# Splitting the next stage's first weight whole before a joint, an output bias as a product, and a longer last run of the down products

## The chip, the cores and the metric

The kernel runs on one core of one Trainium2 chip. The metric is the device time of one execution in microseconds (us); lower is better. The core has a matrix engine (PE), a vector engine (DVE), a scalar engine (ACT), a general engine (POOL) and a queue that only issues transfers (SP). Each takes its own instructions strictly in order, and they wait for one another by semaphores.

## The reference, cut to what matters

One sequence of 256 tokens with 1024 channels passes through two blocks, each of depth two. What follows is cut to the residuals and the parts that the change touches.

```
def rglru_mixer(u, ...):
    ...
    out = (h * ybr) @ w_out + b_out
def conv_ffn(u, w_up, conv_w, conv_b, w_down):
    hcv = causal_dwconv(u @ w_up, conv_w, conv_b)          # 1024 -> 8192
    g, v = hcv[..., :D_FF], hcv[..., D_FF:]
    return (gelu(g) * v) @ w_down                          # 4096 -> 1024
def first_block(x, ...):
    for i in range(2):
        m = ssd_mixer(rmsnorm(x, norm_mix_pre[i]), ...) if i == 0 else rglru_mixer(...)
        x = x + rmsnorm(m, norm_mix_post[i])
        x = x + rmsnorm(conv_ffn(rmsnorm(x, norm_ffn_pre[i]), ...), norm_ffn_post[i])
def second_block(x, c, ...):
    for l in range(2):
        sh1, sc1, gt1, sh2, sc2, gt2 = split(silu(c) @ ada_w[l] + ada_b[l], 6)
        h = rms_norm(x, norm1_g[l]) * (1 + sc1) + sh1
        ...                                                # attention and delta net, merged by gates
        x = x + gt1 * (merged @ w_out[l])
        h = rms_norm(x, norm2_g[l]) * (1 + sc2) + sh2
        x = x + gt2 * (square(relu(h @ w_mlp1[l])) @ w_mlp2[l])
```

## The kernel before, in words

There are eight stages in a row: ssd, ffn0, lru, ffn1, mixer2_0, mlp2_0, mixer2_1, mlp2_1. Between two of them stands a joint, numbered here J1 (ssd to ffn0) to J7 (mixer2_1 to mlp2_1). The 256 tokens are two token tiles of 128, t0 and t1.

Every large product is made in float32 out of three products of split operands (`mm3`, L333 to L335): each factor is cut into a high part and a low part, and high by high, high by low and low by high are added up in PSUM. The weights stream from memory as blocks of 128 x 2048 (`raw`, loaded by SP). A half of a block is a granule: ACT makes its high part (`hi`, L432), DVE its low part (`lo`, L434), which needs the high one. Activations are split the same way (`yh` and `yl`, `xhh` and `xhl`, `hTh` and `hTl`).

A stage ends with its products into four accumulators, acc00 and acc01 for t0 (512 channels each) and acc10 and acc11 for t1. The joint then works on t0 first: residual (L543 to L551 for a normed one, L559 and L560 for a gated one), sum of squares on ACT (L497), inverse root on POOL (`n_ssv` L499, `n_ssr` L503), gain (L517), scale (L520 or L522), eight transposes on PE (`pT`, L531), split into `hTh` and `hTl`. Right behind, PE makes the first product of the next stage for t0 (`ph`, 24 matmuls, L333 to L335), while DVE, ACT and POOL do the same chain for t1. The weight of that first product has four granules, the list `self.ahead`, which `prefetch` splits.

In the two FFNs and the two MLPs `updown` runs over 32 channel tiles: an upward product (`pg` twice, or `pu` once), activation, and later the tile's down products into the accumulators; the products of the last `nl` tiles are made at the end, one accumulator after the other (`out_last`), so that t0's accumulators are done first.

The code is not executed as it stands. A list scheduler orders the instructions of each engine by their dependences and by the place in the code, and `self.after(late, early)` adds an order by hand. A code edit therefore moves instructions elsewhere on an engine's queue too.

Of the kernel before, what the change touches and what calls it, by code (L numbers as in the profile page):

```python
# [17 lines left out]
P = 128  # L18
# [8 lines left out]
# ---------------------------------------------------------------- host layout  # L27
def _chan(a):
    """[C] or [J, C] per-channel values -> [128, J * C / 128], channel = col * 128 + row."""
    a = np.asarray(a)  # L30
    a = a.reshape(-1, P)
    return a.T
# [18 lines left out]
def _kslab(w):  # L51
    """[1024, n] -> [128, 8 * n] with row k * 128 + p at [p, k, :]."""
    n = w.shape[1]
    return w.reshape(KD, P, n).transpose(1, 0, 2).reshape(P, KD * n)


def _ct(w):
    """[k * 128, c] -> [c / 128, 128, k * 128]: one block per 128 columns"""
    r, c = w.shape
    return w.reshape(r // P, P, c // P, P).transpose(2, 1, 0, 3).reshape(c // P, P, r)  # L60


def _pair(a, b=None):
    """blocks two by two: neighbours of a, or a's with b's"""
    if b is None:
        a, b = a[0::2], a[1::2]
    return np.ascontiguousarray(np.concatenate([a, b], 2))


def _nt(w, n):  # L70
    """[1024, c] -> [2 * c / n, 128, 4 * n]"""
    r, c = w.shape
    return np.ascontiguousarray(w.reshape(2, 4, P, c // n, n).transpose(3, 0, 2, 1, 4)).reshape(2 * c // n, P, 4 * n)


def _rt(w):
    """[r, 1024] -> [r / 256, 128, 2 * 1024]"""
# [108 lines left out]
# ---------------------------------------------------------------- kernel  # L186
class Kern:
    def __init__(self, tc, ctx, a, out, at):
# [20 lines left out]
        # the tables are there before the data  # L209
# [5 lines left out]
    def after(self, late, early):  # L215
        """late is issued after early"""
# [32 lines left out]
    def rowload(self, rp, name, eng=None):  # L249
        """one row of 1024 values on all partitions; name is a parameter row or (layer, row of its modulation)"""  # L250
# [5 lines left out]
    # ---- weights  # L256
    def load_par(self, name, eng=None):
        """the per-channel parameters of a stage"""
# [16 lines left out]
    def outpools(self, ctx, name, raw, hi=4):  # L275
        """a stage's own pools for the weights of its last product"""
        return self.pool(ctx, name + "r", raw), self.pool(ctx, name + "h", hi)

    def wload(self, name, i, pool=None, cuts=1):
        """block i of a weight"""  # L280
# [7 lines left out]
    def parts(self, name, i, shape=(8, P), pools=None):  # L288
        """the two halves of block i, each split: [128, *shape] high and low"""
# [9 lines left out]
    def gran(self, raw, shape, pool=None):  # L299
        """one split granule of a weight"""  # L300
# [5 lines left out]
    def ahead_of(self, gen, n):  # L306
        """the same items, each made n items earlier"""
# [22 lines left out]
    def mm3(self, ps, ah, al, bh, bl, first, last):  # L330
        """ps += (ah + al)^T (bh + bl)"""
# [5 lines left out]
    def proj_ch(self, ps, hl, hT):  # L337
        """channels on partitions: ps [128, 256] = w^T h"""
# [4 lines left out]
    def proj_tok(self, ps, hls, hT, t):  # L343
        """tokens on partitions: ps [128, n] = h[tile t] w"""
# [7 lines left out]
    def prefetch(self):  # L352
        """the weights of the next stage's first product"""
        if self.next_head:
# [3 lines left out]
            self.ahead, self.later = [next(self.ahead) for _ in range(2)], self.ahead  # L358

    def head(self, wk, hT, relu2=False, tag="up"):  # L360
        """the first 512 channels of a projection, made with tokens on partitions so that the first token tile
        goes ahead of the second, then transposed: four [128, 256] with channels on partitions"""
# [19 lines left out]
    # ---- small things  # L382
    def rsqrt(self, ss, n, scale, eps, c=""):
        """1 / sqrt(ss * scale + eps), [128, n]"""
# [19 lines left out]
    def softplus(self, x, n):  # L404
        """max(x, 0) + log1p(exp(-|x|)) in place, [128, n]"""
# [24 lines left out]
    def tosplit(self, src, h, l):  # L430
        """h, l = the two exact parts of src"""
# [4 lines left out]
    # ---- between two stages  # L436
    def joint(self, post, pre, first=None):
        """the residual after a stage and the normed, transposed and split input of the next one.
        post: (accumulators, gain row, bias row) for a normed residual, (accumulators, gate row) for a gated one.
        pre: gain row, shift row"""  # L440
        with ExitStack() as ctx:
            jp = self.pool(ctx, "jp", 1, "right")
            xs = []
            for t in range(2):
# [3 lines left out]
                if not post and not t:  # L448
                    # the gain's row goes to all partitions by a product
# [16 lines left out]
            for t in range(2):  # L466
# [8 lines left out]
                if pre:  # L475
                    xn = self.norm(jp, x, *pre_rows)
                    if not t and post:
                        for hl in self.later:
                            if len(post) == 2 or post[1] in ('mix_post1', 'ffn_post0'):
                                self.after(self.lo[-1], self.xg)  # L480
                            self.ahead.append(hl)
                    if t and post:
                        # the first token tile's products go ahead of the second's norm
# [7 lines left out]
    def rnorm(self, jp, halves, scale, eps, name):  # L491
        """1 / sqrt(sum of (scale * halves)^2 + eps)"""
# [13 lines left out]
    def norm(self, jp, x, grow, shrow=None):  # L506
        """rms norm of x times a gain row (plus a shift row)"""
# [17 lines left out]
    def to_chan(self, t, xn, hT):  # L525
        """transposed and split"""
# [8 lines left out]
    def add_normed(self, jp, x, acc, g, b):  # L535
        """x += rms norm of acc (+ bias row) times a gain row"""
# [16 lines left out]
    def add_gated(self, jp, x, acc, gt):  # L553
        """x += gate row * acc"""
# [7 lines left out]
    def out_tok(self, acc, yh, yl, hi, lo, first, last):  # L562
        """acc[t][n] += y[tile t]^T w[:, n half]"""
# [9 lines left out]
    def out_last(self, acc, todo):  # L573
        """the last products into acc, one accumulator after the other"""
# [5 lines left out]
    def conv(self, out, src, taps, shifts, bias=None):  # L580
        """out[:, i] = bias + sum_j taps[j] * src[:, i + shifts[j]], zeros outside; taps[-1] has shift 0"""
# [11 lines left out]
    # ---- first block: SSD  # L593
    def ssd(self, prev):
        nc, tc = self.nc, self.tc
        with ExitStack() as ctx:
# [11 lines left out]
            def blocks():  # L608
                """the input weight's granules in the order of their use"""
# [8 lines left out]
            def chan_block(c0, cb, key, is_z=False, hooks={}):  # L618
                """512 channels from column c0 on: projection, conv, silu"""
# [19 lines left out]
            # dt and the decays  # L639
# [50 lines left out]
            def expo(g, heads):  # L690
                """the exponents, negated: -min(cs_l - cs_s, 0) within a chunk, -(cs_l + cs_s) between the two"""
# [11 lines left out]
            def cbt(g):  # L703
                """C B^T, transposed"""
# [10 lines left out]
            def xtok(g, t):  # L715
                """xs * dt with tokens on partitions"""
# [113 lines left out]
    def updown(self, upper, down, ys, acc, hooks, ada):  # L830
        """32 channel tiles up and down again, the down products a few tiles behind; in the last ones
        the first token tile is finished first"""
        nl, lag = 5, 2
# [16 lines left out]
    # ---- first block: gated conv FFN  # L850
    def ffn(self, prev, l):
        nc = self.nc
        with ExitStack() as ctx:
            self.stage(ctx, f'ffn{l}')
            hT = self.joint(prev, (f'ffn_pre{l}', None))
            px = self.outpools(ctx, "ffn", 2, 5)
# [15 lines left out]
            def upper(cc):  # L872
# [21 lines left out]
                ys[cc] = self.hilo(wk, [P, T], "y", 7)  # L894
# [4 lines left out]
    # ---- first block: RG-LRU  # L899
    def lru(self, prev):  # L900
        nc = self.nc
        with ExitStack() as ctx:
# [16 lines left out]
            def blocks():  # L919
                """the projections by 128 columns: (gate branch or recurrent branch, tile, product)"""  # L920
# [17 lines left out]
            def gates(h, xb, xh, xl):  # L938
# [6 lines left out]
                # a = exp(log_a), 1 - a^2 = -tanh(log_a) (1 + a^2)  # L945
# [4 lines left out]
                # (1 + tanh) * x  # L950
# [5 lines left out]
            def gate_pars():  # L956
                # 4 * log_sigmoid(lambda) = -4 * softplus(-lambda)
# [13 lines left out]
            def finish(*pend):  # L971
                """the last gates, then the root; the exponentials come before it"""
# [10 lines left out]
            for rec, h, ps in blocks():  # L983
                if not rec:
# [20 lines left out]
            acc = self.accs()  # L1005
            todo = []
            for h in range(10):
# [10 lines left out]
                if h < 6:  # L1018
                    self.out_tok(acc, yh, yl, *next(wo), h == 0, False)
# [3 lines left out]
        return acc, 'mix_post1', 'lru_b_out'  # L1023

    # ---- second block
    def ada(self, ctx, rows):
        """rows (layer, row of 6) of the modulation, one channel per partition; the norm gains are folded into
        the scales. One block of 128 channels a step, each held behind the split before it: the vector engine's
        pauses take it in."""
# [36 lines left out]
    def ada_rows(self, l, j0, j1):  # L1066
        """rows j0 to j1 of the modulation, in DRAM"""
# [8 lines left out]
    def mixer2(self, prev, l):  # L1076
        nc = self.nc
        lam0 = 0.8 - 0.6 * math.exp(-0.3 * l)
        with ExitStack() as ctx:
# [6 lines left out]
            def ab(c):  # L1086
                """the accumulators' banks: two for the delta net, two for the attention"""
# [8 lines left out]
            def granules():  # L1096
                """the granules of the projections and the branches in the order of their use"""
# [590 lines left out]
```

## Time and profile before

| what | value |
|---|---|
| median of 3 runs | 1808.29 us (1807.19 to 1811.37) |
| profiled execution | span 1809.0 us, 30091 instructions, within the range of the three runs |
| PE busy | 1732.7 us, 96% of the span |
| DVE busy | 1435.9 us, 79% |
| ACT busy | 990.2 us, 55% |
| POOL busy | 138.6 us, 8% |
| memory read | 360.96 MB, 205 GB/s over the span |
| mean granted TensorE clock | 0.987 of full |

PE is busy nearly all the time, so the time is made of PE's work and of PE's pauses. The pauses stand at the joints and at the starts of stages. The granted clock has two levels, 1.2 and 2.4 GHz, shown as 0.50 and 1.00; after some pauses the profile shows a few us at the lower one.

### The profile page before, as it was taken

Reading aid. Unit: us, or ns where it says so; the run is one execution under the profiler, and the core shown is the slowest. Engines: PE = TensorE matmul, PEld = TensorE weight load, DVE = VectorE, ACT = ScalarE, POOL = GpSimd, SP = SyncE. Lnnn points to the kernel's source line nnn. Section 1 sums busy time; section 2 is a strip of 40 time slices with the busy share of each in tenths; the row PEclk is TensorE's granted clock in tenths of the full one; section 3 lists DMA queues with packets and bytes.
Section 4 is the critical chain, followed back from the end, with each engine's and each line's share of the span. In section 5 each row is a group of like instructions: output and inputs, shape, how many; then the busy total and the mean of one; then the engine's idle time right before and its main releaser. Section 6 shows DMA issues by size and latency. Waiting matters only on the chain.

```text
span 1809.0 us, 30091 instructions
## 1 busy us (share of the span) xinstructions
PE 1732.7 (96%) x11810; PEld 1584.4 (88%) x11810; DVE 1435.9 (79%) x2513; ACT 990.2 (55%) x1687; POOL 138.6 (8%) x190
## 2 busy tenths in 40 slices
PE   8999999999999899999987999999999799999998
PEld 7988789999888699999887989789988798978997
DVE  7788799887788899887789876788768887677554
ACT  5898565555488555555554255545545425446442
POOL 0000100000100100000233000100023210010000
PEclk9999999999999999999999999999999899999999
DMA  7554779774437688764355216899725511477551
GB/s 260 200 177 184 253 290 326 269 271 164 146 143 255 257 312 323 262 237 153 109 188 142 71 48 222 301 359 343 294 89 175 170 48 57 177 283 254 188 187 42
DMA packets 73345, 372.20 MB, mean 206 GB/s; under 512 B 15473, under 2 KB 16929, under 8 KB 40690
## 3 DMA queue, kind: packets, MB, share of 16 engines
q1 hardware_dynamic: 55584, 337.25, 51.9%
q0 software_dynamic: 6576, 22.79, 3.8%
q10 hardware_dynamic: 11042, 10.23, 1.8%
q8 instruction: 93, 1.52, 0.3%
q14 instruction: 50, 0.41, 0.1%
HBM read 360.96 MB, written 9.28 MB: 205 GB/s over the span
## 4 chain that ended last, share of the span: by engine, by line
PE 45%; DVE 9%; DMA 6%; issue 3%; ACT 2%; POOL 1%; ACTq 0%; POOLq 0%; DVEq 0%
PE acc L333 5%; PE acc L334 5%; PE acc L335 5%; PE pg L333 4%; PE pg L335 4%; PE pg L334 4%; PE pu L335 3%; PE pu L334 3%; PE pu L333 3%; DVE lo L434 2%; PE ab L1347 1%; DMA raw<-in_out_dram 1%; ACT hi L432 1%; PE ab L1349 1%; DMA raw<-in_m_dram 1%
## 5 line engine op out<-in xcount | busy, mean ns | idle before, releaser
L432 ACT ACTIVATE hi<-raw 128x1024 fp32r<-128x1024 f32 (+1 forms) x526 | 542.0, 1044 | 434.0 <-PE pg L334 155.4
L434 DVE TENSOR_TENSOR lo<-raw,hi 128x1024 fp32r<-128x1024 f32 (+1 forms) x526 | 631.8, 1210 | 179.4 <-ACT hi L432 176.6
L333 PE MATMUL pg<-hTh,hi 128*128 128x256 f32 x1216 | 345.9, 285 | 0.0
L335 PE MATMUL pg<-hTh,lo 128*128 128x256 f32 x1216 | 345.3, 284 | 0.0
L334 PE MATMUL pg<-hTl,hi 128*128 128x256 f32 x1216 | 345.1, 284 | 0.0
L333 PEld LDWEIGHTS pg<-hTh,hi 128*128 128x128 f32 x1216 | 233.3, 192 | 3.5 <-issue 0.7
L334 PEld LDWEIGHTS pg<-hTl,hi 128*128 128x128 f32 x1216 | 233.3, 192 | 3.0 <-issue 0.7
L335 PEld LDWEIGHTS pg<-hTh,lo 128*128 128x128 f32 x1216 | 233.1, 192 | 1.3 <-issue 1.2
L333 PE MATMUL acc<-hi,yh 128*128 128x512 f32 x512 | 202.7, 396 | 6.0 <-ACT yh L432 6.0
L334 PE MATMUL acc<-lo,yh 128*128 128x512 f32 x512 | 202.1, 395 | 0.0
L335 PE MATMUL acc<-hi,yl 128*128 128x512 f32 x512 | 199.6, 392 | 0.0
L333 PE MATMUL pp<-hTh,hi 128*128 128x256 f32 x576 | 167.8, 291 | 8.0 <-DVE u L590 4.0
L335 PE MATMUL pp<-hTh,lo 128*128 128x256 f32 x576 | 166.4, 289 | 4.0 <-DVE lo L434 4.0
L334 PE MATMUL pp<-hTl,hi 128*128 128x256 f32 x576 | 166.1, 288 | 0.0
L335 PE MATMUL pu<-hTh,lo 128*128 128x256 f32 x448 | 126.9, 283 | 0.0
L333 PE MATMUL pu<-hTh,hi 128*128 128x256 f32 x448 | 126.8, 283 | 0.0
L334 PE MATMUL pu<-hTl,hi 128*128 128x256 f32 x448 | 126.7, 283 | 0.0
L333 PEld LDWEIGHTS pp<-hTh,hi 128*128 128x128 f32 x576 | 112.6, 195 | 11.8 <-issue 5.4
L333 PEld LDWEIGHTS acc<-hi,yh 128*128 128x128 f32 x512 | 97.3, 190 | 24.6 <-ACT yh L432 7.6
L1054 DVE CUSTOM_DVE_ANT_0 ada_w<-ada_w,c_row 128x1024 f32<-128x1024 f32 x96 | 115.7, 1218 | 3.0 <-DMA ada_w<-in_ada_dram 3.0
L335 PEld LDWEIGHTS pp<-hTh,lo 128*128 128x128 f32 x576 | 112.6, 196 | 5.8 <-DVE lo L434 5.2
L335 PEld LDWEIGHTS acc<-hi,yl 128*128 128x128 f32 x512 | 96.9, 190 | 21.7 <-DVE yl L434 0.6
(450 smaller groups left out, 3437.6 us busy)
## 6 DMA issues: line engine op xcount, KB each, us to landing
raw<-in_up_dram SPq DMA_DIRECT2D x60, 1024.0 KB, 5.2
raw<-in_m_dram SPq DMA_DIRECT2D x60, 1024.0 KB, 7.0
ada_w<-in_ada_dram SPq DMA_DIRECT2D x96, 512.0 KB, 5.0
raw<-in_down_dram SPq DMA_DIRECT2D x32, 1024.0 KB, 5.6
raw<-in_ssd_in_dram SPq DMA_DIRECT2D x19, 1024.0 KB, 5.9
raw<-in_dn_dram SPq DMA_DIRECT2D x16, 1024.0 KB, 4.9
raw<-in_gate_dram SPq DMA_DIRECT2D x16, 1024.0 KB, 5.0
raw<-in_att_dram SPq DMA_DIRECT2D x16, 776.0 KB, 4.4
```

The lines of the kernel that those rows point to most:

```text
L333: mm(ps, ah, bh, start=first, stop=False)
L334: mm(ps, ah, bl, start=False, stop=False)
L335: self.mm = mm(ps, al, bh, start=False, stop=last)
L432: self.hi = self.nc.scalar.activation(h, src, AF.Copy)
L434: self.lo.append(self.nc.vector.tensor_tensor(l, src, h.bitcast(F32), op=ALU.subtract))
L1054: self.after(nc.vector.tensor_tensor_reduce(out=raw, in0=raw, in1=act, scale=0.5, scalar=0.0, op0=ALU.mult, op1=ALU.add, accum_out=col[:, ...
L1347: nc.tensor.matmul(pd[:, i * P:(i + 1) * P], Dt[:, 4 * q + i, :], Y[:, i, :], start=True, stop=True)
L1349: nc.tensor.matmul(pe[:, i * P:(i + 1) * P], Y[:, i, :], Dt[:, 4 * q + i, :], start=True, stop=True)
```

## The change

Three edits, each in its own place; the rest of the file's difference is comments taken out, which moves the line numbers by some lines.

First, `prefetch` now makes all four granules of the next stage's first weight where it stands. Before, it made two, and the other two were made inside the joint of t0, behind the gain.

Second, the output bias of the recurrent stage (lru). Before, a row of 1024 values went to all partitions, and DVE added it to the accumulators in the joint (L544, four adds). Now the bias is loaded as 2 x 512, split, and multiplied by a 2 x 128 selector: eight matmuls open the four accumulators, and the joint gets no bias.

Third, in `updown` the last run has 7 tiles instead of 5 and the down products stand 3 tiles behind instead of 2, with 7 instead of 5 buffers for down weights and 9 instead of 7 for activations.

```diff
@@ prefetch
-            self.ahead, self.later = [next(self.ahead) for _ in range(2)], self.ahead
+            self.ahead = list(self.ahead)
@@ joint
                     xn = self.norm(jp, x, *pre_rows)
-                    if not t and post:
-                        for hl in self.later:
-                            if len(post) == 2 or post[1] in ('mix_post1', 'ffn_post0'):
-                                self.after(self.lo[-1], self.xg)
-                            self.ahead.append(hl)
@@ updown
-        nl, lag = 5, 2
+        nl, lag = 7, 3
@@ ffn and mlp2
-            px = self.outpools(ctx, "ffn", 2, 5)
+            px = self.outpools(ctx, "ffn", 2, 7)
...
-                ys[cc] = self.hilo(wk, [P, T], "y", 7)
+                ys[cc] = self.hilo(wk, [P, T], "y", 9)
@@ lru, in the loop over the projections
+                if rec and h == 4:
+                    raw = sq[0:2, 8:10, :].rearrange("p a n -> p (a n)")
+                    o = self.rat['lru_b_out']
+                    nc.gpsimd.dma_start(out=raw, in_=self.a['rows'][o:o + 1, :].rearrange("o (a n) -> (o a) n", a=2))
+                    brow = [wk.tile([P, 512], F32R, name="hu", tag="hu", bufs=2)[0:2] for _ in range(2)]
+                    self.tosplit(raw, *brow)
+                    sel = wk.tile([2, 2, P], F32R, name="sel")
+                    nc.scalar.activation(sel, self.ident[0:2, 0:2].unsqueeze(2).broadcast_to([2, 2, P]), AF.Copy)
@@ lru, before the output products
+            for t in range(2):
+                for n in range(2):
+                    for i in range(2):
+                        nc.tensor.matmul(acc[t][n], sel[:, n, :], brow[i], start=i == 0, stop=False)
...
-                    self.out_tok(acc, yh, yl, *next(wo), h == 0, False)
+                    self.out_tok(acc, yh, yl, *next(wo), False, False)
@@
-        return acc, 'mix_post1', 'lru_b_out'
+        return acc, 'mix_post1', None
```

What the scheduler makes of it is shown at three places.

**The start of ffn0, ACT's queue.** `G` and `V` are the gate and value of a channel tile, `yh` the high part of its result, `hi` a weight's high part; the numbers of `raw` tell the blocks apart. Before:

```order
L432 ACTIVATE hi_3036<-raw_2938 128x1024
L432 ACTIVATE hi_3131<-raw_3129 128x1024
L892 ACT_TABLE_LOAD
L892 ACTIVATE G_2639<-G_2639 128x256
L586 ACTIVATE G_2653<-pht_2609,par_2429 128x256
L586 ACTIVATE V_2657<-pht_2610,par_2429 128x256
L586 ACTIVATE G_2704<-pg_2679,par_2429 128x256
L432 ACTIVATE yh_2649<-V_2643 128x256
L432 ACTIVATE hi_2711<-raw_2709 128x1024
```

Now:

```order
L432 ACTIVATE hi_3113<-raw_3018 128x1024
L432 ACTIVATE hi_3208<-raw_3206 128x1024
L432 ACTIVATE hi_3301<-raw_3206 128x1024
L887 ACT_TABLE_LOAD
L887 ACTIVATE G_2639<-G_2639 128x256
L581 ACTIVATE G_2653<-pht_2609,par_2437 128x256
L581 ACTIVATE V_2657<-pht_2610,par_2437 128x256
L581 ACTIVATE G_2704<-pg_2679,par_2437 128x256
L432 ACTIVATE hi_2711<-raw_2709 128x1024
L432 ACTIVATE yh_2649<-V_2643 128x256
```

Two more weight halves stand ahead of the first `yh`: the second half of the third down block (raw_3206) and one of an up block (raw_2709). On PE the first accumulator product, which needs that `yh`, still stands right behind the products of channel tile 2 (`pg`), ahead of those of tile 3:

```order
L335 MATMUL pg<-hTh,lo 128x256
L333 MATMUL acc_2576<-hi,yh 128x512
L333 MATMUL pg<-hTh,hi 128x256
L334 MATMUL pg<-hTl,hi 128x256
L335 MATMUL pg<-hTh,lo 128x256
```

**The tail of lru, DVE's queue.** `s` is the recurrence's result of a head, `xhl` its low part, which the output product needs; raw_6683 before and raw_6698 now are the second block of the next stage's first weight (`up_h`). Before:

```order
L1013 TENSOR_TENSOR s_6712<-s_6712,yb_5687 128x256
L1012 SCALAR_TENSOR_TENSOR s_6726<-tt_5686,gx_5685 128x256
L434 TENSOR_TENSOR lo_6734<-raw_6719,hi_6733 128x1024
L434 TENSOR_TENSOR xhl_6716<-s_6712,xhh_6715 128x256
L1013 TENSOR_TENSOR s_6726<-s_6726,yb_5687 128x256
L434 TENSOR_TENSOR xhl_6730<-s_6726,xhh_6729 128x256
L544 TENSOR_TENSOR xb_6808<-acc00_6519,rowb_6802 128x512
L544 TENSOR_TENSOR xb_6808<-acc01_6520,rowb_6802 128x512
```

Now:

```order
L1022 TENSOR_TENSOR s_6735<-s_6735,yb_5687 128x256
L434 TENSOR_TENSOR lo_6709<-raw_6698,hi_6708 128x1024
L434 TENSOR_TENSOR lo_6713<-raw_6698,hi_6712 128x1024
L434 TENSOR_TENSOR xhl_6739<-s_6735,xhh_6738 128x256
L1021 SCALAR_TENSOR_TENSOR s_6749<-tt_5686,gx_5685 128x256
L434 TENSOR_TENSOR lo_6757<-raw_6742,hi_6756 128x1024
L1022 TENSOR_TENSOR s_6749<-s_6749,yb_5687 128x256
L434 TENSOR_TENSOR xhl_6753<-s_6749,xhh_6752 128x256
L543 SCALAR_TENSOR_TENSOR xn_6828<-acc00_6526,rowb_6823 128x512
```

The two low parts of the `up_h` block left the joint and stand ahead of the low parts of the last two heads; the adds of the bias row are gone.

**The joint J7, DVE's queue** (J5 reads the same). The first row is the gate times acc00; `lo<-raw,hi` twice is the second block of the MLP's first weight. Before:

```order
L559 TENSOR_TENSOR xn<-acc_17387,rowb 128x512
L560 TENSOR_TENSOR x<-x,xn 128x512
L517 TENSOR_TENSOR xn<-x,rowb 128x512
L559 TENSOR_TENSOR xn<-acc_17388,rowb 128x512
L560 TENSOR_TENSOR x<-x,xn 128x512
L517 TENSOR_TENSOR xn<-x,rowb 128x512
L434 TENSOR_TENSOR lo<-raw,hi 128x1024 x2
L522 SCALAR_TENSOR_TENSOR xn<-xn,n_ssr,rowb 128x512 x2
```

Now:

```order
L554 TENSOR_TENSOR xn<-acc_17394,rowb 128x512
L434 TENSOR_TENSOR lo<-raw,hi 128x1024 x2
L555 TENSOR_TENSOR x<-x,xn 128x512
L554 TENSOR_TENSOR xn<-acc_17395,rowb 128x512
L512 TENSOR_TENSOR xn<-x,rowb 128x512
L555 TENSOR_TENSOR x<-x,xn 128x512
L512 TENSOR_TENSOR xn<-x,rowb 128x512
L517 SCALAR_TENSOR_TENSOR xn<-xn,n_ssr,rowb 128x512 x2
```

The two low parts moved from behind the sixth row to behind the first, ahead of t0's residual.

## Rows read from the trace of the kernel before

**Rows 1.** The page's busy time: us, share of the span, instructions.

```profile
PE 1732.7 (96%) x11810; PEld 1584.4 (88%) x11810; DVE 1435.9 (79%) x2513; ACT 990.2 (55%) x1687; POOL 138.6 (8%) x190
```

**Rows 2.** Stretches: length, busy us by engine, granted clock, DMA share, GB/s.

```profile
300.00:345.00 45.00, 45.00 (x322) 42.51 (x321) 41.15 (x66) 25.09 (x37) 0.00 (x0) 1.00 0.82 288
234.20:241.00 6.80, 5.94 (x16) 4.78 (x17) 5.97 (x12) 4.18 (x9) 0.00 (x0) 0.50 0.77 311
568.70:572.10 3.40, 2.94 (x8) 1.97 (x7) 3.40 (x5) 3.40 (x6) 0.00 (x0) 0.50 0.12 15
602.80:606.20 3.40, 3.31 (x12) 2.74 (x13) 2.99 (x7) 1.86 (x5) 0.00 (x0) 0.50 0.81 335
630.10:633.50 3.40, 3.40 (x11) 2.73 (x10) 3.40 (x6) 1.34 (x4) 0.00 (x0) 0.50 0.78 317
```

**Rows 3.** PE's timeline at joints and starts: start, us, instruction, wait and releaser.

```profile
197.54 0.71 PE L777 MATMUL prb<-ident,rs_y 128*128 128x128 f32 x4 [1.03 <-POOL rs_y L390]
...
235.06 0.80 PE L333 MATMUL acc<-hi,yh 128*128 128x512 f32 x1 [2.82 <-ACT yh L432]
...
494.53 1.09 PE L531 MATMUL pT<-ident,xn 128*128 128x128 f32 x8 [1.34 <-DVE xn L520]
...
567.81 1.38 PE L333 MATMUL acc<-hi,xhh 128*128 128x512 f32 x4 [1.81 <-ACT hi L432]
...
602.89 1.97 PE L531 MATMUL pT<-ident,xn 128*128 128x128 f32 x8 [4.29 <-DVE xn L520]
612.51 1.07 PE L531 MATMUL pT<-ident,xn 128*128 128x128 f32 x8 [1.36 <-DVE xn L520]
...
628.78 0.50 PE L333 MATMUL acc<-hi,yh 128*128 128x512 f32 x1 [2.45 <-ACT yh L432]
...
1156.24 1.32 PE L531 MATMUL pT<-ident,xn 128*128 128x128 f32 x8 [0.49 <-DVE xn L522]
...
1351.11 0.45 PE L335 MATMUL pa<-hi,hTl 128*128 128x388 f32 x1 [1.08 <-DVE hTl L434]
...
1619.20 1.32 PE L531 MATMUL pT<-ident,xn 128*128 128x128 f32 x8 [1.52 <-DVE xn L522]
```

**Rows 4.** SP's and ACT's timelines at the start of ffn0.

```profile
223.54 0.33 SPq L285 DMA_DIRECT2D raw<-in_down_dram  x1
...
230.55 1.06 ACT L432 ACTIVATE hi<-raw 128x1024 fp32r<-128x1024 f32 x1 [1.24 <-DMA raw<-in_down_dram]
```

**Rows 5.** ACT's timeline at the start of ffn1.

```profile
627.37 1.06 ACT L432 ACTIVATE hi<-raw 128x1024 fp32r<-128x1024 f32 x1 [1.04 <-DMA raw<-in_up_dram]
628.33 0.40 ACT L432 ACTIVATE yh<-V 128x256 fp32r<-128x256 f32 x1
```

**Rows 6.** ACT's, DVE's and PE's timelines at the tail of lru and in J3.

```profile
588.44 2.01 ACT L432 ACTIVATE hi<-raw 128x1024 fp32r<-128x1024 f32 x2 [1.52 <-DMA raw<-in_up_h_dram]
...
593.18 1.39 DVE L544 TENSOR_TENSOR xb<-acc,rowb 128x512 f32<-128x512 f32 x2 [0.67 <-PE acc L335]
...
596.63 0.39 PE L334 MATMUL acc<-lo,xhh 128*128 128x512 f32 x1
...
598.22 0.39 PE L335 MATMUL acc<-hi,xhl 128*128 128x512 f32 x1
```

**Rows 7.** ACT's (J5, then J7), DVE's and POOL's timelines (J7).

```profile
1149.41 2.01 ACT L432 ACTIVATE hi<-raw 128x1024 fp32r<-128x1024 f32 x2 [5.89 <-DMA raw<-in_m_h_dram]
...
1611.82 2.01 ACT L432 ACTIVATE hi<-raw 128x1024 fp32r<-128x1024 f32 x2 [5.97 <-DMA raw<-in_m_h_dram]
...
1611.15 0.69 DVE L559 TENSOR_TENSOR xn<-acc,rowb 128x512 f32<-128x512 f32 x1 [3.87 <-DMA rowb<-mod]
...
1615.27 2.35 DVE L434 TENSOR_TENSOR lo<-raw,hi 128x1024 fp32r<-128x1024 f32 x2
...
1615.87 1.83 POOL L499 TENSOR_SCALAR n_ssv<-n_ss 128x1 f32<-128x1 f32 x1 [15.46 <-ACT junk L497]
...
1624.64 0.30 POOL L499 TENSOR_SCALAR n_ssv<-n_ss 128x1 f32<-128x1 f32 x1 [6.28 <-ACT junk L497]
```

More of the change, by code (lines that the diff above doesn't have):

```diff
@@ L1623, in mlp2 @@
             hT = self.joint(prev, ((l, 4), (l, 3)))
-            px = self.outpools(ctx, "mlp", 2, 5)
+            px = self.outpools(ctx, "mlp", 2, 7)
             wk = self.pool(ctx, f"mlp{l}", 3)
@@ L1649, in upper @@
                     nc.vector.tensor_tensor(Y, R, R, op=ALU.mult)
-                ys[cc] = self.hilo(wk, [P, T], "y", 7)
+                ys[cc] = self.hilo(wk, [P, T], "y", 9)
                 self.tosplit(Y, *ys[cc])
```

## The prediction

> **What bounds the kernel now.** I read the page's busy times first: PE works 1732.7 of 1809.0 us [rows 1], so its pauses are worth 76.3 us in all, and DVE with 79% has slack on average only. Next the stretches: in the middle of ffn0 PE is busy 45.00 of 45.00 us at the full clock [rows 2]. The steady parts of the FFNs are pure PE work, and no order of other engines can shorten them. What is left is PE's timeline with its waits [rows 3], of which the reader is to see two kinds. At a joint `pT` waits for DVE's `xn`: 4.29 us at J3, 1.52 at J7, 1.34 at J2, only 0.49 at J5. At a start the first accumulator product waits for a part that ACT makes: 2.82 us in ffn0, 1.81 in lru, 2.45 in ffn1. Last the granted clock: behind those three starts and J3 a stretch stands at 0.50, 1.2 GHz, for 3.4 us (6.8 in ffn0) [rows 2]. After the pauses of 1.34 and 1.52 us none is seen.
>
> **How the working goes.** Every term is the change of a pause of PE, or of a stretch at the low clock, against the profiled execution. Its span of 1809.0 us lies 0.7 above the median of the three runs and among them; I apply the sum to the median.
>
> **The steady parts: 0.** Three tiles of distance instead of two, and more buffers, give room to an engine that is late. PE is not waiting there, so there is nothing to win, and the number of products is the same. The cover is PE's own queue. The end of the kernel has no following joint and stays too.
>
> **J1: +1.0.** In the built order the last low half of the `up_h` block moves ahead, but three accumulator products instead of six stand on PE between the sums of squares and the broadcast `prb` that waits for POOL, 1.03 us today [rows 3]. Three products at 0.227 us (eight products start 1.59 us from first to last [rows 6]) are 0.7 us less cover. A second low half, 1.18 us (half of the 2.35 for two [rows 7]), is now the last DVE work ahead of the joint. Bounds 0 and +1.9; I take about the middle.
>
> **Start of ffn0: +2.6.** PE's first accumulator product waits for the first `yh`, and on ACT two more halves now stand ahead of it, 1.0 us each (two took 2.01 [rows 6]): +2.0. One belongs to the third down block. Its load was issued at 223.54 and ACT got it at 230.55, 7.0 us later [rows 4]; the buffer comes free one low half later now, which makes the landing up to 1.2 us later. Bounds +2.0 and +3.2. The tile 3 products, which the larger distance puts ahead of the rest of the down products, could cover this. But the single accumulator product stands ahead of them on PE, so they wait too. Whoever is late next is tile 1's `yh`, behind the same queue and hidden by 24 `pg` products.
>
> **J2 and J4: -0.9.** J2's two low halves leave t0's chain, and the last run of seven tiles has 42 products of t1, 9.5 us at 0.227, behind t0's accumulators. So t0's wait, 1.34 us at J2 [rows 3], can go. But t1's chain starts at the accumulators' end as before and sets the joint's length next. Bounds 0 and -1.3 for J2, and I take -0.4; -0.5 for J4, which has the same form.
>
> **Start of lru: -1.7.** The eight bias products, 1.8 us at 0.227, need nothing late and fit into the 1.81 us that PE waits for the first weight part [rows 3]: they cost nothing. If that cover failed they would cost 1.8. With PE at work there, the stretch at 1.2 GHz from 568.70 on [rows 2] should not come: half of 3.4 us. Bounds 0 and -1.7. The bias's own small load and split lie in the middle of lru under PE's work.
>
> **J3: -2.0.** The adds (1.39 us [rows 6]) and two low halves leave t0's chain. Today it runs from 593.18 [rows 6] to 602.89 [rows 3], 9.7 us; without them 6.0. It doesn't start as early, though: on DVE the two low halves now stand ahead of the parts of the last two heads, and wait for high halves made from 588.44 on [rows 6]. PE is fed with t1's products meanwhile, and only 11 products remain behind t0's last one. They end at 598.60 (602.89 less 4.29 [rows 3]), so t0 is done at 598.60 - 2.5 = 596.1 and `pT` starts at 602.1 instead of 602.89: -0.8. For t1 the wait of 1.36 us goes almost, since its adds fall away too: -1.2. The pause at t0 stays 3.5 us long, and so does the low clock behind it. Bounds 0 (the last heads come too late for PE) and -5.6 (both waits go).
>
> **Start of ffn1: -3.2.** Today `yh` at 628.33 stands behind a high half that waited 1.04 us for its load and took 1.06 [rows 5]. Now `yh` stands ahead of it: the 2.45 us pause falls to about 0.9, -1.5, and behind so short a pause I expect no stretch at 1.2 GHz: -1.7 more. Bounds 0 and -3.8.
>
> **J6: -1.0.** A small instruction that stood ahead of `hTl` on DVE stands behind it now; the wait was 1.08 us [rows 3]. Bounds 0 and -1.1.
>
> **J5 and J7: +2.1 and +1.6, and +0.65 each for the clock.** This is the costliest place. The two low halves stand behind the first gated product and ahead of t0's whole residual, and their high halves wait for a load: ACT starts them at 1149.41 and 1611.82 [rows 7]. At J7 the low halves run from 1612.87 (one high half later) to 1615.2; four DVE instructions of about 0.7 us (0.69 [rows 7]) follow, till 1618.1. From there to `pT` it was 1.25 us to `n_ssv` (1614.6 to 1615.87) and 3.33 from there, of which 1.53 were `n_ssv` itself stretched beside the low halves (1.83 against 0.30 [rows 7]): without that 3.05, so `pT` at 1621.2, +2.0. ACT's squares no longer wait behind its high halves, which I estimate to save 0.4 of the 1.25, hence +1.6. At J5 everything comes 462.41 us earlier (1149.41 for 1611.82 [rows 7]): `pT` at 1158.75 instead of 1156.24, +2.5, less the same 0.4, hence +2.1. The pauses become 2.6 and 3.1 us, longer than the 2.45 that a stretch at 1.2 GHz followed. Its price: eight transposes took 1.97 us at J3 at the low clock and 1.32 at J7 [rows 3], 0.65 more, and behind them PE waits for `hTh` and `hTl` anyway. Bounds 0 and 1.7 each.
> The Trainium skill, TensorE: Matmul & The Clock Gate, HAM oscillation, charges throttled time at half its length; by that J5 and J7 would cost 1.7 each in clock, and the sum would be +1.9, 1810.2 us. The row above speaks for less, since PE is not busy throughout.
>
> **Sum.** 1.0 + 2.6 - 0.9 - 1.7 - 2.0 - 3.2 - 1.0 + 2.1 + 1.6 + 1.3 = -0.2 us: 1808.1 us. About 0.2%, 3.6 us, is what a measurement of this kernel can tell from no change.
>
> **The rivals.** *The splits are free, faster.* If the MLP's first weight lands some 3 us earlier, the low halves fall into DVE's idle time ahead of the joint, 3.87 us at J7 [rows 7], and J5 and J7 cost nothing: -5.0. If ffn0's start also costs only 1 us, -1.6 more: 1801.5. For it: DVE is idle just there. Against it: ACT waited 5.9 us for that load, and the change doesn't touch it. 33 in 100, together with a J3 near its far bound, 3.6 us lower than my term and about 1804.5 alone.
> *The clock eats it, slower.* The low clock is not avoided at the starts of lru and ffn1 (+3.4), and the new pauses at J5 and J7 cost full stretches (+2.1): 1813.6. It decides from two of these four on together with ffn0 at +3.2. For it: behind a pause of 1.81 us the clock fell. Against it: PE has products to do in both starts. 25 in 100.
> *Nothing happens.* The joints' length is set by t1's chain behind the last product, which the change hardly shortens; the gains and the new waits are then both near 0, and the time is 1808.3. It ends as my forecast does, within 0.2%; both together have 42 in 100.
>
> **How the numbers follow.** Forecast and the third rival give "same", 0.42, with 1805 to 1811.5 as their own range from the bounds of ffn0, J3 and the clock taken one at a time. The first rival gives "faster", 0.33, the second "slower", 0.25. The range for 8 in 10 reaches from the first rival's 1801.5 to the second's 1813.6.
>
> **What would show each step right or wrong.** Right: no pause over 0.5 us at the start of lru, with the granted clock at 1.00 behind it; a pause of about 5.4 us ahead of ffn0's first accumulator product, with one product and then 24 `pg` behind; `pT` of J5 and J7 2.6 and 3.1 us after the accumulators' end, with two low halves in front of the residual; a pause near 1 us at ffn1; J3's `pT` still 3.5 us late. Wrong: low halves at J5 and J7 that end before the accumulators of t0, a J3 pause under 1.5 us, or a stretch at 0.50 where I expect none. The forecast fails as a whole if the steady parts gain, that is if the middle of an FFN, counted from its first accumulator product to its last, gets shorter by more than the starts explain.

## The result, and the profile after

The changed kernel takes 1833.28 us (median of 4 runs, 1830.33 to 1835.02) against 1807.74 of before (4 runs, 1800.18 to 1811.37). The ratio is 1.0139, 95% interval 1.012 to 1.0158: 25 us slower, where I forecast no change and named 1813.6 as the upper end. The page's head of the profiled execution:

```profile
span 1833.2 us, 30105 instructions
...
PE 1746.0 (95%) x11818; PEld 1596.7 (87%) x11818; DVE 1427.0 (78%) x2510; ACT 990.9 (54%) x1689; POOL 126.8 (7%) x190
```

PE does eight matmuls more than in [rows 1] and is busy 13.3 us longer; the span is 24.2 us longer, so its pauses grew by 10.9. Next, PE's timeline at the same places as [rows 3], and at J4 and J6, where before there was no wait for t0 worth a row:

```profile
199.55 0.71 PE L772 MATMUL prb<-ident,rs_y 128*128 128x128 f32 x4 [0.77 <-POOL rs_y L390]
...
240.75 0.80 PE L333 MATMUL acc<-hi,yh 128*128 128x512 f32 x1 [3.85 <-ACT yh L432]
...
504.17 1.97 PE L526 MATMUL pT<-ident,xn 128*128 128x128 f32 x8 [5.85 <-DVE xn L515]
...
576.73 2.12 PE L1014 MATMUL acc<-hu,sel 2*128 2x512 f32 x8
...
612.72 1.97 PE L526 MATMUL pT<-ident,xn 128*128 128x128 f32 x8 [3.55 <-DVE xn L515]
...
621.73 1.03 PE L526 MATMUL pT<-ident,xn 128*128 128x128 f32 x8
...
637.07 0.50 PE L333 MATMUL acc<-hi,yh 128*128 128x512 f32 x1 [1.26 <-ACT yh L432]
...
900.20 1.97 PE L526 MATMUL pT<-ident,xn 128*128 128x128 f32 x8 [6.88 <-DVE xn L517]
...
1174.79 1.32 PE L526 MATMUL pT<-ident,xn 128*128 128x128 f32 x8 [1.96 <-DVE xn L517]
...
1182.98 1.29 PE L526 MATMUL pT<-ident,xn 128*128 128x128 f32 x8 [0.84 <-DVE xn L517]
...
1366.02 1.97 PE L526 MATMUL pT<-ident,xn 128*128 128x128 f32 x8 [3.55 <-DVE xn L517]
...
1643.26 1.31 PE L526 MATMUL pT<-ident,xn 128*128 128x128 f32 x8 [2.42 <-DVE xn L517]
...
1651.45 1.29 PE L526 MATMUL pT<-ident,xn 128*128 128x128 f32 x8 [0.82 <-DVE xn L517]
```

The three pauses that are new, or longer than before, are at 504.17 (J2, 1.34 before), 900.20 (J4) and 1366.02 (J6): 5.85, 6.88 and 3.55 us, 16.3 in all, where t0 should have been ready long ahead. All three stand behind a stage that `updown` makes. Behind each, the eight transposes take 1.97 us, and a first stretch at the low clock follows; columns of the stretches as in [rows 2]:

```profile
300.00:345.00 45.00, 45.00 (x313) 42.09 (x312) 44.17 (x72) 25.54 (x38) 0.00 (x0) 1.00 0.90 326
504.10:510.10 6.00, 5.93 (x20) 4.59 (x21) 5.33 (x10) 2.53 (x6) 1.70 (x4) 0.61 0.18 70
900.20:906.20 6.00, 6.00 (x24) 5.54 (x25) 5.59 (x9) 2.64 (x6) 1.25 (x4) 0.62 0.13 53
1366.00:1372.00 6.00, 5.98 (x21) 5.52 (x22) 5.49 (x9) 2.64 (x6) 0.41 (x2) 0.50 0.16 62
```

The steady part of ffn0, the first row, is as full as before. Why is `xn` late at J2? First the list of waits on SP's queue between 480 and 505 us: who waited, for whom, us in total, times, longest:

```profile
SPq L446 <- PE acc L335: 14.4, 1, 14.4
```

SP's timeline, where that transfer and the one of t1 are issued at last, and the same two in the kernel before, some 280 us ahead of J2, as J1 writes the rows that they read:

```profile
496.31 0.81 SPq L446 DMA_DIRECT2D x<-xd  x2
```

```profile
211.15 7.07 SPq L446 DMA_DIRECT2D x<-xd  x2
```

And DVE's, where the sum with the residual waits for it:

```profile
490.74 1.29 DVE L543 SCALAR_TENSOR_TENSOR xn<-acc,rowb 128x512 f32<-128x512 f32 x2 [6.85 <-DMA rowb<-in_rows_dram]
...
499.74 1.41 DVE L546 SCALAR_TENSOR_TENSOR x<-xn,pn_ssr,x 128x512 f32<-128x512 f32 x2 [7.71 <-DMA x<-xd]
```

The load of the residual `x`, a transfer that depends on nothing in this stage's products, waits 14.4 us for an accumulator product of line 335, high by low. That product reads the low activation tile `yl`. The only tie between the two is the place in memory. The addresses of the built programs, in bytes of a partition, say it:

```
                           before              changed
ffn0's own tiles      153760 to 178336    170144 to 198816   (top: the last yl, 197792 to 198816)
modulation's tiles    178336 to 194720    198816 to 215200
J2's tiles            198624 to 229344    198624 to 229344   (bottom: x of t0, 198624 to 202720)
```

Two more weight buffers (16384 bytes, high and low) and two more activation buffers (4096) push the stage up. Its top tile now reaches 192 bytes into the joint's first, so the joint can't load its residual until the last product has read that tile. The modulation's tiles (for the reference's `silu(c) @ ada_w[l]`, which the kernel makes in these stages) lie in the joint's space now too; but so they do in experiment 3 (196768 to 213152), where the three pauses are gone.

At J4 and J6 something else ends the wait. ACT's timeline at J4 and then at J6:

```profile
893.36 0.27 ACT L1082 ACTIVATE ada_r<-padaT 24x128 f32<-24x128 f32 x1 [13.00 <-PE padaT L1080]
893.53 0.57 ACT L492 ACTIVATE junk<-acc 128x512 f32<-128x512 f32 x1
...
1362.51 0.27 ACT L1082 ACTIVATE ada_r<-padaT 32x128 f32<-32x128 f32 x1 [16.88 <-PE padaT L1080]
...
1362.68 0.61 ACT L492 ACTIVATE junk<-x 128x512 f32<-128x512 f32 x1
```

And PE's, what they wait for:

```profile
892.92 0.40 PE L1080 MATMUL padaT<-ident,acol 128*24 128x128 f32 x2
...
1362.06 0.41 PE L1080 MATMUL padaT<-ident,acol 128*32 128x128 f32 x2
```

A small copy of the modulation's transposes, `ada_r`, stands on ACT ahead of t0's square `junk`, and its `padaT` stands on PE behind the last accumulator products. So ACT waits 13.0 and 16.9 us with t0's square behind it, and PE can do t0's transposes only after that square. In the order of the kernel before, `ada_r` stands behind t0's transposes; experiment 3 shows the rows. The load at J4 is late as well (890.99, after 13.9 us for the same kind of product); the one at J6 is not (1345.25, 20.8 us ahead of t0's transposes). There the top tile is `Y`, the squared value, which no product reads.

### The profile page after: what moved, and what is told of

It is laid out like the page before. It is cut to its first block, busy times and chain, and to the rows that moved or that the text cites. A ratio compares the mean times of both kernels' runs of the same rounds, so it can differ in the third digit from the quotient of the medians.

```text
span 1833.2 us, 30105 instructions
## 1 busy us (share of the span) xinstructions
PE 1746.0 (95%) x11818; PEld 1596.7 (87%) x11818; DVE 1427.0 (78%) x2510; ACT 990.9 (54%) x1689; POOL 126.8 (7%) x190
## 4 chain that ended last, share of the span: by engine, by line
PE 47%; DVE 8%; DMA 6%; ACT 3%; issue 1%; ACTq 0%; POOL 0%; SPq 0%; DVEq 0%; POOLq 0%
PE acc L334 5%; PE acc L333 5%; PE acc L335 4%; PE pg L333 4%; PE pg L335 4%; PE pg L334 4%; PE pu L333 3%; PE pu L334 3%; PE pu L335 3%; DVE lo L434 3%; DMA raw<-in_att_dram 1%; ACT hi L432 1%; DMA raw<-in_out_dram 1%; DMA raw<-in_m_h_dram 1%; DMA raw<-in_m_dram 1%
```

## The experiments

Theory A: the larger buffers, through the space that they take, make the three pauses. Theory B: the whole split does. Theory C: the longer last run and the larger distance do, by the order of products. Each experiment names its time, and, where timed, the ratio to the kernel before on the same chip.

**1. The third edit undone.**

```diff
-        nl, lag = 7, 3
+        nl, lag = 5, 2
-... "ffn", 2, 7), "mlp", 2, 7), "y", 9)
+... "ffn", 2, 5), "mlp", 2, 5), "y", 7)
```

> The changed kernel with the third edit undone: last run 5, distance 2, 5 weight buffers, 7 activation buffers; the whole split ahead of the joint and the bias product stay. Theory A (the larger buffers reach into the space of the joint's tiles, whose loads and squares then wait for the last products at J2, J4 and J6): the three waits of PE for t0's transposes, 5.85, 6.88 and 3.55 us in the changed kernel, fall below 1.5 each, and the time to about 1814 us (1833 less the 18.9 us that the changed kernel's timeline loses at these three joints). Theory B (the whole split ahead of the joints costs the time): the time stays at 1828 to 1833 us.

1807.83 us, ratio 1.0005 (0.999 to 1.0021). PE's timeline at J2, J4 and J6 shows no wait:

```profile
489.74 1.03 PE L526 MATMUL pT<-ident,xn 128*128 128x128 f32 x8
...
876.59 1.03 PE L526 MATMUL pT<-ident,xn 128*128 128x128 f32 x8
...
1336.96 1.03 PE L526 MATMUL pT<-ident,xn 128*128 128x128 f32 x8
```

Theory B falls. The first two edits together cost nothing that can be measured; the third costs all 25 us, more than the 18.9 that I expected.

**2. The buffers alone.** The larger pools of the change, with last run 5 and distance 2 as before, so that no product needs them.

```diff
-        nl, lag = 7, 3
+        nl, lag = 5, 2
```

> The changed kernel with last run 5 and distance 2 as before, but with the 7 weight buffers and 9 activation buffers of the change: nothing uses the additional room. Theory A: J2, J4 and J6 wait as in the changed kernel, the sum of the three waits is over 12 us, time 1826 to 1833 us. Theory C (the longer last run and the larger distance, that is the order of the products, make the waits): the waits are those of before, time about 1814 us.

1830.43 us, ratio 1.0119 (1.0096 to 1.0142). The pauses are those of the changed kernel:

```profile
504.05 1.97 PE L526 MATMUL pT<-ident,xn 128*128 128x128 f32 x8 [5.55 <-DVE xn L515]
...
899.02 1.97 PE L526 MATMUL pT<-ident,xn 128*128 128x128 f32 x8 [6.87 <-DVE xn L517]
...
1361.51 1.97 PE L526 MATMUL pT<-ident,xn 128*128 128x128 f32 x8 [3.55 <-DVE xn L517]
```

Theory C falls: room that no product needs is enough.

**3. Eight activation buffers.** The whole change, less one buffer (in the FFNs and the MLPs).

```diff
-                ys[cc] = self.hilo(wk, [P, T], "y", 9)
+                ys[cc] = self.hilo(wk, [P, T], "y", 8)
```

> The changed kernel with 8 activation buffers instead of 9 in the FFNs and MLPs, and nothing else: the stage's own tiles then end at byte 196768 of a partition instead of 198816, below the joint's first tile at 198624. Theory A: an overlap of 192 bytes with the last low activation tile makes the loads late, so the waits at J2, J4 and J6 go (sum under 4 us instead of 16.3) and the time is about 1814 us. Theory C: the time stays at 1828 to 1833 us.

1813.21 us, ratio 1.003 (1.0015 to 1.0044): 2048 bytes give back 20.1 us. The pauses at J2, J4 and J6 are gone:

```profile
494.01 1.03 PE L526 MATMUL pT<-ident,xn 128*128 128x128 f32 x8
...
885.14 1.03 PE L526 MATMUL pT<-ident,xn 128*128 128x128 f32 x8
...
1344.78 1.03 PE L526 MATMUL pT<-ident,xn 128*128 128x128 f32 x8
```

So is the early `ada_r`. This is the built order on ACT at J4, of the changed kernel and then of this one (`hTh` is made from t0's transposes, `junk` are squares):

```
L492 ACTIVATE junk,pn_ss<-acc_6949 128x512
L1082 ACTIVATE ada_r<-padaT 24x128
L492 ACTIVATE junk,pn_ss<-acc_6950 128x512
L492 ACTIVATE junk,n_ss<-x 128x512
...
L492 ACTIVATE junk,pn_ss<-acc_6952 128x512
L432 ACTIVATE hTh<-pT 128x4x128 x2
L1082 ACTIVATE ada_r<-padaT 24x128
L492 ACTIVATE junk,n_ss<-x 128x512
```

Where the changed kernel has the row between the two halves of t0's first square, this one has it behind t0's transposes; the code that writes these instructions is the same. The 5.4 us that stay above experiment 1 show at a new place, the tails of the two FFNs, where PE waits for the last tile's `yh`:

```profile
479.38 0.50 PE L333 MATMUL acc<-hi,yh 128*128 128x512 f32 x1 [2.44 <-ACT yh L432]
...
868.25 0.80 PE L333 MATMUL acc<-hi,yh 128*128 128x512 f32 x1 [3.03 <-ACT yh L432]
```

On ACT, a part of the next stage's weight stands ahead of the last tile's gate there, and in ffn0's tail it waits for its load:

```profile
472.41 1.06 ACT L432 ACTIVATE hi<-raw 128x1024 fp32r<-128x1024 f32 x1 [3.51 <-DMA raw<-in_lru_h_dram]
```

**4. The third edit alone**, on the kernel before (the diff of `updown`, the pools and `ys` as in the change).

> The kernel before with the third edit alone (last run 7, distance 3, 7 and 9 buffers). Theory A: the three waits are there as in the changed kernel, time 1826 to 1833 us. Theory B: the time is that of before, 1804 to 1812 us.

1829.42 us, ratio 1.0113 (1.0091 to 1.0135), with waits of 7.78, 6.86 and 3.75 us. This agrees with theory A from the other side.

**5. Two granules for the MLPs.** Experiment 1, and ahead of the MLPs' joints the split as before.

```diff
-            self.ahead = list(self.ahead)
+            m = 2 if name.startswith('m1') else 4
+            self.ahead, self.later = [next(self.ahead) for _ in range(m)], self.ahead
...
+                    if not t and post:
+                        for hl in self.later:
+                            if len(post) == 2 or post[1] in ('mix_post1', 'ffn_post0'):
+                                self.after(self.lo[-1], self.xg)
+                            self.ahead.append(hl)
```

> The kernel of the first experiment (third edit undone), in which the weights that go into the two MLPs are split as before: two granules ahead, two inside the joint behind the gain; at the other five joints the whole split stays ahead. Theory A1 (at J5 and J7 the two low halves, which wait for a late load, hold up t0's residual; pauses 2.34 and 2.84 us in the first experiment, and 0.85 and 0.70 for t1): the pauses return to 0.5 and 1.5 us, the time falls by about 4.7 us, from 1807.8 to 1803. Rival (the pauses there are given back later): the time stays at 1806 to 1809 us.

1805.41 us, ratio 0.9981 (0.9973 to 0.999). Against experiment 1 that is 0.24% or 4.3 us by the ratios, 2.4 by the medians, between the 1803 of the theory and the 1806 of the rival. t0's pauses at J5 and J7:

```profile
1153.20 1.32 PE L532 MATMUL pT<-ident,xn 128*128 128x128 f32 x8 [0.94 <-DVE xn L523]
...
1613.89 1.83 PE L532 MATMUL pT<-ident,xn 128*128 128x128 f32 x8 [2.05 <-DVE xn L523]
```

In experiment 1 they were 2.34 and 2.84, and 0.85 and 0.70 for t1, which has none here: 3.7 us less. It is the one version here whose interval lies below the kernel before, by 0.1 to 0.3%.

**6. The bias product alone**, on the kernel before.

> The kernel before with the second edit alone, the bias of the recurrent stage as a product. Theory: the pause of 1.81 us at the start of that stage's output products is filled, the adds of 1.39 us leave J3's chain of t0 and of t1, the time falls by 2 to 4 us, to 1803 to 1805 us. Rival (the products cost what they fill, and J3 is set by other work): 1806 to 1808 us.

1807.56 us, ratio 0.9999 (0.9985 to 1.0012): the expectation failed. The pause of 1.81 us is filled, but by eight products that take 2.1 us themselves, which is no gain; the stretch at the low clock comes all the same (a granted clock of 0.59 over the 3.4 us from 569.00; the last section shows experiment 1, where it is the same); J3's pause falls from 4.29 to 3.48 us, too little for the measurement to tell from no change.

**7. The split alone**, on the kernel before.

> The kernel before with the first edit alone, the whole split ahead of every joint. Theory: the pauses at J2 and J4 fall by about 1 us each, those at J5 and J7 grow by 4.7 us in all, net 1 to 3 us slower than before, 1808 to 1810 us. Rival (the split alone is a gain at every joint): 1803 to 1805 us.

1809.24 us, ratio 1.0009 (0.9998 to 1.002). J2's pause of 1.34 us is gone, those of J5 and J7 are 2.17 and 2.98 us. The direction fits the theory's net of +1 to +3 us; the interval still holds no change.

**8. Eight buffers and two granules.** Experiment 3 with the first edit undone.

> The kernel with eight activation buffers (the third experiment) with the first edit undone: last run 7, distance 3, bias product, two granules split ahead and two in the joint. Theory D (what the longer last run and the larger distance still cost there, 5.4 us over the first experiment, are the waits of 2.44 and 3.03 us for the last tile's high part in the tails of the two FFNs, behind a weight part that waits for its load): these waits stay above 2 us each, and only J5 and J7 improve, time 1808 to 1811 us. Theory E (the whole split makes those waits): they go too, time 1803 to 1806 us.

1809.24 us, ratio 0.9995 (0.998 to 1.001). The tails still wait:

```profile
477.78 0.59 PE L333 MATMUL acc<-hi,yh 128*128 128x512 f32 x1 [1.83 <-ACT yh L432]
...
870.97 0.79 PE L333 MATMUL acc<-hi,yh 128*128 128x512 f32 x1 [3.05 <-ACT yh L432]
```

So the whole split doesn't make the tails; the first of them fell a little under the 2 us that I had named. They come with the third edit only where nothing overlaps: in the changed kernel and in experiments 4, 9 and 10, with the same last run and distance, PE doesn't wait there, nor in experiment 1 without that edit. What in the edit makes them is not separated. The time lies where theory D put it.

**9. Eight buffers and a dead tile.** Nothing writes or reads it; it moves the tiles above it up by 2048 bytes.

```diff
             wk = self.pool(ctx, f"ffn{l}", 3)
+            wk.tile([P, 512], F32, name="pad", tag="pad", bufs=1)
```

(and the same for the MLPs, on the kernel of experiment 3)

> The kernel with eight activation buffers, 1813 us, and ahead of them in the stage's space a tile of 2048 bytes that nothing writes or reads: the number of buffers and all work stay, only the addresses above it move up by 2048, so that the last low activation tile again ends at byte 198816, 192 above the joint's first tile. Theory A (it is the place, not the number of buffers): the waits at J2, J4 and J6 return, 5 to 7, 7 and 3.5 us, and the time is 1826 to 1833 us. Rival (the ninth buffer lets other work run ahead and that makes the waits): the time stays at 1811 to 1815 us.

1827.84 us, ratio 1.0106 (1.0089 to 1.0122). PE at J2, J4 and J6:

```profile
500.99 1.65 PE L526 MATMUL pT<-ident,xn 128*128 128x128 f32 x8 [3.74 <-DVE xn L515]
...
895.96 1.97 PE L526 MATMUL pT<-ident,xn 128*128 128x128 f32 x8 [6.87 <-DVE xn L517]
...
1361.33 1.82 PE L526 MATMUL pT<-ident,xn 128*128 128x128 f32 x8 [3.55 <-DVE xn L517]
```

The waits on SP's queue between 478 and 503 us:

```profile
SPq L446 <- PE acc L335: 12.3, 1, 12.3
```

It is the place, not the number of buffers. J2's pause came back smaller than the 5 us that I expected, the other two as expected.

**10. Nine buffers at the low end.** The whole change; only the addresses of `y` are taken first, so that the value tiles `V` of the convolution lie on top.

```diff
+            for _ in range(9):
+                self.hilo(wk, [P, T], "y", 9)
```

(and the same for the MLPs, where `Y` lies on top with or without it)

> The changed kernel with all its nine activation buffers, but these at the lower end of the stage's tiles; the value tiles of the convolution lie at the upper end instead, 192 bytes into the joint's first tile. Their last reader is done some 15 us earlier. Theory A1 (the late load of the residual makes the wait at J2, a square that stands behind the last transposes of the modulation on ACT makes those at J4 and J6, and in the built order it stands there here too): the wait at J2 falls under 1 us, those at J4 and J6 stay near 6.9 and 3.6, time about 1823 to 1828 us. Rival (the late loads make all three waits): all three go, about 1813 us.

1823.11 us, ratio 1.0081 (1.0057 to 1.0104). SP issues J2's residual at 480.14 instead of 496.31. SP's timeline:

```profile
480.14 0.81 SPq L446 DMA_DIRECT2D x<-xd  x2
```

And the pauses part, in PE's:

```profile
495.21 1.09 PE L526 MATMUL pT<-ident,xn 128*128 128x128 f32 x8 [0.67 <-DVE xn L515]
...
889.85 1.97 PE L526 MATMUL pT<-ident,xn 128*128 128x128 f32 x8 [6.93 <-DVE xn L517]
...
1354.44 1.78 PE L526 MATMUL pT<-ident,xn 128*128 128x128 f32 x8 [3.55 <-DVE xn L517]
```

So the overlap costs in two ways. The transfer itself waits, which makes J2. And the scheduler puts `ada_r` ahead of t0's square: in all five kernels with the 192 bytes of overlap (the changed one, experiments 2, 4, 9 and 10) it stands there at J4 and J6; in the seven kernels without them (before and experiments 1, 3 and 5 to 8) it stands behind t0's transposes. That goes with the pauses at J4 and J6; at J4 the transfer is early here (868.63 instead of 890.99), and the pause stays. The order is read from the built programs and the traces. Why the scheduler makes it was not opened up, and no run moved `ada_r` alone, so this second way is argued from ACT's order and its waits.

The overlap also costs at the start of ffn0. The order with two more weight halves ahead of the first `yh` is made in the same five kernels, with pauses of 3.70 to 4.13 us. In experiment 3 only one more half stands there and the pause is 1.95 us; the dead tile of experiment 9 brings the other half back, and 3.89 us.

**11. The kernel before, once more.**

> The kernel before, unchanged, profiled once more. Theory F (the wait of 2.45 us at the start of ffn1 and of 2.82 us at the start of ffn0 in its first profile came from loads that were late in that one execution; every later kernel, also those with one edit alone, shows 1.0 to 1.5 at ffn1): ffn1's wait is 1.0 to 1.6 us and no stretch at 1.2 GHz follows it, ffn0's is 1.5 to 2.5. Rival (the change's order of ACT's queue made the gain there): ffn1's wait is 2.3 to 2.6 us again.

1806.09 us, a single run. PE's waits at the starts of ffn0 and ffn1:

```profile
236.04 0.50 PE L333 MATMUL acc<-hi,yh 128*128 128x512 f32 x1 [1.63 <-ACT yh L432]
...
625.40 0.50 PE L333 MATMUL acc<-hi,yh 128*128 128x512 f32 x1 [1.47 <-ACT yh L432]
```

They were 2.82 and 2.45 in [rows 3]. The stretch from 626 to 630 us stands at the full clock. Two of my terms rested on waits of one execution.

## Why the prediction was wrong, step by step

**The step that failed** is "The steady parts: 0", where it says that more buffers give room to an engine that is late. I costed the buffers as room in time and not as room in memory: no term, no bound and no rival asked whose tiles lie where the pools grow. Experiments 1, 2, 3 and 9 show that this alone makes 15 to 23 of the 25 us by the medians: 20.1 between the changed kernel and experiment 3, 14.6 between experiments 3 and 9, and 22.6 between experiments 1 and 2. Not all of it is pauses: with as many matmuls, PE is busy 1746.0 us in the changed kernel and 1739.0 in experiment 3, at mean granted clocks of 0.980 and 0.984, which is 7.0 of the 19.5 us between the two spans. The rest of that step holds: PE is busy 45.00 of 45.00 us in the middle of ffn0 after as in [rows 2].

**J2, J4 and J6** (-0.9 and -1.0) went the other way for that reason. Without the overlap the reasoning on J2 was right, and too cautious: in experiments 1 and 7 its 1.34 us go altogether. At J4 there was no wait for t0 to take away before, only 0.82 us for t1, which stay in experiment 1; the -0.5 rested on no row. J6's wait for `hTl` is gone in the changed kernel, but stays without the overlap: 1.07 us in experiments 1 and 7, 0.47 in 3.

**The tails of the FFNs** were missing. With eight buffers and no overlap, PE waits 2.44 and 3.03 us there (experiment 3): it is through with the upward products before ACT and DVE have made the last activation. I had called PE's queue the cover; in that tail it is too short. Why the kernels with the overlap don't wait there is open.

**Start of ffn0, +2.6**: the pause is 3.85 us. Against 2.82 that is +1.0, against the 1.63 of the second profile of before +2.2. The base was of one execution. The mechanism held for the order that was built, but that order too comes only with the overlap (3.70 to 4.13 us against 1.95 in experiment 3 and 1.62 to 1.66 in experiments 1, 6 and 7): most of this term is the same step again. **Start of ffn1, -3.2**: 1.26 us and the full clock came as forecast, but the kernel before does the same (1.47, full clock) in its second profile; the change gives next to nothing.

**Start of lru, -1.7**: no pause, as forecast, but the low clock came in spite of PE's work. The term is 0, and experiment 6 finds no gain.

**J3, -2.0** is right in its parts: 3.55 us for t0 (forecast 3.5), none for t1.

**J5 and J7**: forecast pauses 2.6 and 3.1 us, measured 1.96 and 2.42, with 0.84 and 0.82 at t1 that I had not forecast, and no low clock behind (eight transposes in 1.32 and 1.31 us); in experiment 5, behind 2.05 us at J7, they took 1.83 and the 3.4 us from there have a granted clock of 0.53. The length of the pause alone doesn't decide, as I had assumed. Together 4.0 us over [rows 3] against 5.0 forecast; experiment 5 gives 3.7 of pauses back. The mechanism is right. **J1, +1.0**: the pause is 0.77 instead of 1.03, so the term was wrong by its size and sign.

**The price of the low clock**: at J2 the way from t0's to t1's transposes is 8.78 us (504.17 to 512.95) in the changed kernel and 7.44 (494.01 to 501.45) in experiment 3, 1.3 us more. By the half of throttled time that the Trainium skill, TensorE: Matmul & The Clock Gate, HAM oscillation, charges, the stretch at 0.61, that is 4.7 of 6.0 us at the low level, would cost 2.3, an estimate. The measurement lies between that and my 0.65.

**The rivals.** The time came out on the side of "The clock eats it, slower", but not by it: of its four terms, ffn1's 1.7 us stayed away, J5 and J7 kept the full clock, lru's low clock was there before too, and ffn0's start, +2.2 at most, is all that is left. The low clock that is new stands mostly elsewhere, behind the pauses of J2, J4 and J6. None of the three rivals names what happened.

## What to carry to other kernels

More buffers cost memory before they give time: where pools of one stage and tiles of the next share space, compare the addresses, and look in the built order for a load that waits for an engine it has no data from. A pool that reaches a few hundred bytes too far, here 192, can cost more than a new order of the products gains. And a wait from a single profile is a sample: profile the kernel before twice if a term rests on it.

## What the runs showed of the hardware that I had not expected

The granted clock fell while PE had no long pause. In experiment 1 PE runs the eight bias products, which have two rows of the 128, and goes on with hardly a wait; stretches with columns as in [rows 2]:

```profile
564.10:567.40 3.30, 2.99 (x7) 2.41 (x8) 3.30 (x6) 3.30 (x4) 0.00 (x0) 0.50 0.95 324
560.70:562.80 2.10, 2.10 (x10) 1.43 (x9) 1.12 (x3) 2.00 (x5) 1.10 (x2) 1.00 0.00 0
```

And PE's timeline there:

```profile
560.69 2.13 PE L1014 MATMUL acc<-hu,sel 2*128 2x512 f32 x8
...
564.41 0.79 PE L334 MATMUL acc<-lo,xhh 128*128 128x512 f32 x1 [0.47 <-DVE lo L434]
```

PE is busy all of the 2.10 us at the full clock, has one pause of 0.47 us, and stands at 1.2 GHz from 564.1 to 567.4. In the changed kernel the same stretch is 580.5 to 583.8, at 0.50 with PE busy 3.30 of 3.30 us. Before, a pause of 1.81 us stood in the place of these products, and the clock fell as well. Why it fell here is open: no run separates the eight small products from the pause of 0.47 us behind them.

Also, executions of one order differ: the first products into the accumulators start at 118.36 us in the profile of before and at 123.09 in that of the changed kernel, with the same order on PE up to there, as a weight load landed some 3 us later. Some 4 us of a single pair of profiles are therefore not the change's.
